# Stick-breaking attention inside a decoder layer: which short scans and which projection piece stand behind the current head's transpositions

## The chip, the cores and the metric

The kernel runs on one core of a Trainium2 chip. The metric is device time in microseconds (us) of one execution, as the median of several runs. Five engines work side by side, each through its own list of instructions in a fixed order: TensorE (PE in the profile; its weight loads are PEld), VectorE (DVE), ScalarE (ACT), GpSimd (POOL) and SyncE (SP), which issues the transfers. An instruction that waits holds up all that stand behind it in its engine's list.

## The reference

One layer of a hybrid decoder on 1024 positions of width 1024: a mixing sub-layer (stick-breaking attention with 16 heads of 64, a Mamba-2 mixer, two gates), a cross-attention into 256 memory tokens and a feed-forward. The change touches the stick-breaking attention alone:

```
z = einsum('bhtd,bhsd->bhts', q / 8, k)          # s < t only
log_1mb = where(causal, log_sigmoid(-z), 0)
tail = cumsum(log_1mb, axis=s, reverse=True)
w = where(causal, exp(z + tail), 0)
o = einsum('bhts,bhsd->bhtd', w, v)
```

With n = sigmoid(-z), the weight of a key s is the running product of n from the diagonal down to s+1, less the product down to s. So a query row needs one running product over its keys, taken from the diagonal towards key 0, and no logarithm.

## The kernel before

**Tiles.** A head's 1024 queries are eight blocks b = 0 to 7 of 128. Blocks 0 to 3 are the head's first half, 4 to 7 its second. Block b has keys 0 to 128(b+1). Per block, in `scores` (L923): TensorE multiplies queries and keys (L935, L936, tile `sc`), ScalarE takes the sigmoid into a tile `n` (L937), and VectorE runs one `tensor_tensor_scan` over the whole row in place (L939), 128 to 1024 elements long, so that a scan's width tells its block: 256 and 384 are blocks 1 and 2, 896 is block 6.

**Values.** For each half, `values` (L944) goes over key blocks i (4 in the first half, 8 in the second). `tr(i)` transposes the four query blocks' columns of key block i on TensorE into one PSUM tile `tr` of 512 columns (L953); ScalarE subtracts one and rounds to the high part `wth` (L956); VectorE makes the low part `wtl` (L957, kept in `lows[h, half, i]`). Three steps later `av(i)` adds both parts' products with the values into the PSUM tile `av` (L965, L966). After the last key block ScalarE copies `av` out (`oT`, L969).

**Buffers that bind.** There are two `tr` tiles, so `tr(2)` needs that `wtl` of key block 0 has read its tile. There is one `av` tile, so the first product of a half waits for the copy `oT` of the half before. In the first half the last key blocks hold only part of the queries: key block 2 is 256 wide and key block 3 is 128 wide.

**Projections.** Beside this, TensorE computes the q and k projections of heads further on, 128 columns at a time for two heads, in pieces of three matmuls of 512 columns (L126 to L128; `dense`, L847). A projection has sixteen pieces, eight for each half of the positions, and `(half, kk)` names one. The second half of an even head has the first eight pieces of a k projection beside it, that of an odd head the first eight of a q projection.

**Order.** The lists are not written in final order: the code is traced in the order that `interleave` (L983) gives, and a scheduler places the instructions, from due times and costs, under the ties that the code adds. `behind` (L218) ties an instruction's issue behind another of the same engine, and `issue_behind` (L213) adds such a tie afterwards. Two stand here before: each projection piece stands behind a product eight marks back (L861), and the scan of block 6 stands behind the low part of key block 2 of the same head's first half (L938). While a head's second half runs, VectorE also gets the scans of the next head's first half.

Of the kernel before, what the change touches and what calls it, by code (L numbers as in the profile page):

```python
# [16 lines left out]
P = 128  # L17
# [6 lines left out]
C_Q, C_K, C_V, C_Z = 0, 1024, 2048, 3072  # L24
# [30 lines left out]
def hybrid_block(ctx, tc, a, out, dbg=None):  # L55
    nc = tc.nc
    V, A, T = [InTurn(tc, e) for e in (nc.vector, nc.scalar, nc.tensor)]
# [12 lines left out]
    def mk(pl, shape, dt, tag, bufs=None):  # L70
        uid[0] += 1
        kw = {} if bufs is None else {"bufs": bufs}
        return pl.tile(shape, dt, tag=tag, name=f"{tag}_{uid[0]}", **kw)
# [57 lines left out]
    def load_split(wp, src, shape, rb=3, eng=None):  # L131
        raw = mk(wp, shape, F32, "wraw", bufs=rb)
        nc.sync.dma_start(raw, src)
        hi = mk(wp, shape, F32R, "whi")
        lo = mk(wp, shape, F32R, "wlo")
        hi_sb(hi, raw, eng)
        lo_of(lo, raw, hi)
        return hi, lo

    def colblock(w, c0, n=P):  # L140
        return w[:, c0:c0 + n].rearrange("(k p) f -> p k f", p=P)
# [3 lines left out]
    ident = mk(cp, [P, P], F32, "ident")  # L145
# [67 lines left out]
    def issue_behind(ins, mark):  # L213

        tc.add_manual_dep(ins.ins, mark.ins.name,
                          mybir.DependencyInfo(mybir.DependencyClass.NoSync, mybir.DependencyReason.DATA), reason="order")

    def behind(marks):  # L218

        st = ExitStack()  # L220
        for m in marks:
            st.enter_context(tc.issue_after(m.ins))
        return st
# [52 lines left out]
    with ExitStack() as pa:  # L276
# [24 lines left out]
        with ExitStack() as p1:  # L301
# [135 lines left out]
            pt = mk(psp, [P, HALF], F32, "pdt", bufs=1)  # L437
# [4 lines left out]
            pt = mk(psp, [P, HALF], F32, "pv")  # L442
# [382 lines left out]
        with ExitStack() as p2:  # L825
# [14 lines left out]
            V.memset(mask, 0.0)  # L840
            G.affine_select(mask[:, S - P:], mask[:, S - P:], [[-1, P]], ALU.is_gt, 1.0, base=0, channel_multiplier=1)

            marks, sig, highs, lows = [], [], [], {}
            PIN = 8
            FQ = 1

            def dense(c0, evac):  # L847

                st = {}

                def first():
                    st["w"] = load_split(wp, colblock(w_in, c0), [P, KT, P], 1)

                def part(half, kk):
                    def run():
                        if kk == 0:
                            st["ps"] = mk(psm, [P, HALF], F32, "mm")
                        whi, wlo = st["w"]
                        for k in range(kk * FQ, kk * FQ + FQ):
                            ins = mm3(st["ps"], whi[:, k, :], wlo[:, k, :], *hT(k, half), k == 0, k == KT - 1)  # L860
                            if k == kk * FQ and len(marks) >= PIN:  # L861
                                issue_behind(ins, marks[-PIN])
                        if kk == KT // FQ - 1:
                            evac(st["ps"], half)
                    return run

                return [first] + [part(half, kk) for half in range(2) for kk in range(KT // FQ)]
# [3 lines left out]
            def qk_proj(hp):  # L871
                for j in range(2):
                    heads[2 * hp + j] = {}

                def rooms(half, *names):
                    if half == 0:
                        for n in names:
                            for j in range(2):
                                heads[2 * hp + j][n] = mk(qk, [P, S], F32R, n)
                    sl = slice(half * HALF, (half + 1) * HALF)  # L880
                    return [heads[2 * hp + j][n][:, sl] for n in names for j in range(2)]

                def move(dst, src):
                    nc.sync.dma_start(dst.bitcast(F32), src.bitcast(F32))

                def ev_q(ps, half):
                    q0, q1 = rooms(half, "qs")
                    low = mk(t2, [P, HALF], F32R, "gt")  # L890
                    A.activation(q0, ps, AF.Copy)
                    A.activation(q1[HD:P], ps[HD:P], AF.Copy)
                    V.tensor_tensor(low, ps, q0.bitcast(F32), ALU.subtract)
                    move(q0[HD:P], low[0:HD])
                    move(q1[0:HD], low[HD:P])

                def ev_k(ps, half):
                    h0, h1, l0, l1 = rooms(half, "kh", "kl")
                    low = mk(t2, [P, HALF], F32R, "gt")
                    A.activation(h0, ps, AF.Copy)  # L900
                    A.activation(h1[HD:P], ps[HD:P], AF.Copy)
                    V.tensor_tensor(low, ps, h0.bitcast(F32), ALU.subtract)
                    move(h0[HD:P], h0[0:HD])
                    move(h1[0:HD], h1[HD:P])
                    for j, l in enumerate((l0, l1)):
                        for r in (l[0:HD], l[HD:P]):
                            move(r, low[j * HD:(j + 1) * HD])

                return dense(C_Q + hp * P, ev_q), dense(C_K + hp * P, ev_k)

            def gate_proj(gi):
                def ev(ps, half):
# [10 lines left out]
            def scores(h, half, tb, ns_):  # L923
                def run():
                    hd = heads[h]
                    if half == 0 and tb == 0:
                        values_of(h)
                    b = half * 4 + tb
                    L = (b + 1) * P
                    nt = mk(bp, [P, (half + 1) * HALF], F32, f"n{half}")  # L930
                    ns_.append(nt)
                    for s0 in range(0, L, HALF):
                        s1 = min(L, s0 + HALF)
                        ps = mk(psc, [P, HALF], F32, "sc")[:, :s1 - s0]
                        T.matmul(ps, hd["qs"][:, b * P:(b + 1) * P], hd["kh"][:, s0:s1], start=True, stop=False)  # L935
                        marks.append(T.matmul(ps, hd["qs"][:, b * P:(b + 1) * P], hd["kl"][:, s0:s1], start=False, stop=True))  # L936
                        sig.append(A.activation(nt[:, s0:s1], ps, AF.Sigmoid, scale=-(HD ** -0.5)))  # L937
                    with behind([lows[h, 0, 2]] if b == 6 else []):  # L938
                        V.tensor_tensor_scan(nt[:, 0:L][:, ::-1], nt[:, 0:L][:, ::-1], mask[:, S - L:][:, ::-1], 1.0, ALU.mult, ALU.max)  # L939
                return run  # L940

# [2 lines left out]
            def values(h, half, ns_):  # L944

                st = {}
                ni = 4 * (half + 1)

                def tr(i):
                    t0 = max(0, i - 4 * half)  # L950
                    pt = mk(pst, [P, HALF], F32, "tr")
                    for tb in range(t0, 4):
                        T.transpose(pt[:, tb * P:(tb + 1) * P], ns_[tb][:, i * P:(i + 1) * P], ident)  # L953
                    wh = mk(wt, [P, HALF], F32R, "wth")
                    wl = mk(wt, [P, HALF], F32R, "wtl")
                    highs.append(A.activation(wh[:, t0 * P:], pt[:, t0 * P:], AF.Identity, bias=mone))  # L956
                    lows[h, half, i] = V.scalar_tensor_tensor(wl[:, t0 * P:], pt[:, t0 * P:], -1.0, wh[:, t0 * P:].bitcast(F32), ALU.add, ALU.subtract)  # L957
                    st[i] = (wh, wl, t0 * P)

                def av(i):  # L960
                    if i == 0:
                        st["po"] = mk(psv, [P, HALF], F32, "av")
                    po, vt = st["po"], heads[h]["v"]
                    wh, wl, off = st[i]
                    T.matmul(po[:, off:], vt[:, i, :], wh[:, off:], start=i == 0, stop=False)  # L965
                    marks.append(T.matmul(po[:, off:], vt[:, i, :], wl[:, off:], start=False, stop=i == ni - 1))  # L966
                    if i == ni - 1:
                        o = mk(t2, [P, HALF], F32, "oT")
                        A.activation(o, po, AF.Copy)  # L969
                        for j in range(2):  # L970
                            nc.sync.dma_start(o_d[j][h * HD:(h + 1) * HD, half * HALF:(half + 1) * HALF], o[j * HD:(j + 1) * HD])

                def step(i):
                    def run():
                        if i < ni:
                            tr(i)
                        if i >= LAG:
                            av(i - LAG)
                    return run

                return [step(i) for i in range(ni + LAG)]
# [21 lines left out]
            ns_ = {m: [] for m in range(NM)}  # L1003
# [3 lines left out]
            for m in range(NM):  # L1007
                h, half = m // 2, m % 2
                hp, r = m // 4, m % 4
# [21 lines left out]
    with ExitStack() as p3:  # L1031
# [36 lines left out]
        marks = []  # L1068
# [411 lines left out]
    marks = []  # L1480
# [815 lines left out]
```

## Time and profile before

| | |
|---|---|
| median of 3 runs | 2502.8 us (2500.87 to 2503.42) |
| profiled execution, its own time from first to last instruction | 2498.5 us |
| attention stage, from the first scan to the last transposition | 660.4 to 1075.8 us of the span |
| two heads, from a scan of 896 at 851.64 us to the next but one at 901.06 us | 49.4 us |
| TensorE busy, 850 to 900 us | 48.71 of 50 us |
| VectorE busy, 850 to 900 us | 38.13 of 50 us |
| ScalarE busy, 850 to 900 us | 30.70 of 50 us |
| GpSimd busy, 850 to 900 us | 1.05 of 50 us |

The profiled execution has no time but its span; the runs' median lies 4.3 us above it. A row of the timeline gives start, length, engine, line, operation, the tile written and the tile read, the shapes, how many were merged, and in brackets how long the engine was idle before and what released it. Matmuls overlap: a 512-column matmul is listed with 0.39 us, and the next one starts 0.23 us after it. Instructions on VectorE and ScalarE also overlap by about 0.1 us.

### The profile page before, as it was taken

The numbers are of one execution on the slowest core, as the hardware profiler recorded it, in microseconds if no ns is written. First come the engines' busy times: TensorE is split into PE (matmuls) and PEld (weight loads), VectorE is DVE, ScalarE is ACT, GpSimd is POOL, SyncE is SP. The second block draws the span as 40 slices with busy tenths as digits, with TensorE's granted clock in tenths as the row PEclk, the third lists the DMA queues.
The fourth block names the chain that finished last, engine by engine and source line by source line (L and its number), as shares of the span: only waits on it lengthen the run. The fifth ranks groups of instructions, "written<-read, shape, count | busy, mean of one in ns | idle before, by whom it ended". The sixth has DMA issues, their size and how long they took to land. (4 is left out here: it accounts for less than half of the span.)

```text
span 2498.5 us, 33391 instructions
## 1 busy us (share of the span) xinstructions
PE 2438.4 (98%) x12306; PEld 2010.1 (80%) x12306; DVE 1807.4 (72%) x2261; ACT 1167.0 (47%) x2072; POOL 604.5 (24%) x505
## 2 busy tenths in 40 slices
PE   7999999999999999989999999999999999999998
PEld 5888788888788888877777778888888888888887
DVE  7767877767577777689888774577468556566997
ACT  5344455555465665566644312344335333344433
POOL 3221645443000000134444141102012322220001
PEclk9999999999999999999999999999999999999999
DMA  7565443333444334366332481321242322334322
GB/s 250 180 219 184 156 147 102 110 101 93 131 110 110 102 103 109 103 193 206 115 97 78 138 278 62 126 96 51 93 143 68 101 76 79 98 94 170 125 102 101
DMA packets 253741, 312.40 MB, mean 125 GB/s; under 512 B 17535, under 2 KB 169608, under 8 KB 253450
## 3 DMA queue, kind: packets, MB, share of 16 engines
q1 hardware_dynamic: 253290, 309.22, 38.8%
q8 instruction: 97, 1.59, 0.3%
q10 hardware_dynamic: 288, 1.05, 0.1%
q14 instruction: 66, 0.54, 0.1%
HBM read 210.59 MB, written 82.84 MB: 117 GB/s over the span
## 5 line engine op out<-in xcount | busy, mean ns | idle before, releaser
L939 DVE TENSOR_TENSOR_SCAN n<-n,mask 128x128 f32<-128x128 f32 (+7 forms) x128 | 170.0, 1350 | 27.7 <-ACT n L937 24.4
L123 DVE TENSOR_TENSOR sw<-sf,sw 128x512 fp32r<-128x512 f32 x142 | 127.0, 898 | 71.4 <-ACT sw L120 69.3
L120 ACT ACTIVATE sw<-sf 128x512 fp32r<-128x512 f32 x142 | 88.9, 628 | 157.4 <-PE mm L231 140.2
L956 ACT ACTIVATE wth<-tr,mone 128x512 fp32r<-128x512 f32 x192 | 110.7, 585 | 100.5 <-PE tr L953 100.1
L957 DVE SCALAR_TENSOR_TENSOR wtl<-tr,wth 128x512 fp32r<-128x512 f32 x192 | 101.8, 546 | 58.4 <-ACT wth L956 58.3
L732 DVE SCALAR_TENSOR_TENSOR b<-b,prmT,b 128x1023 f32<-128x1023 f32 (+2 forms) x72 | 110.5, 1534 | 16.9 <-ACT b L726 16.3
L123 DVE TENSOR_TENSOR sw<-wr,sw 128x512 fp32r<-128x512 f32 x107 | 98.8, 924 | 26.2 <-ACT sw L120 25.9
L230 PE MATMUL mm<-h,sw 128*128 128x512 f32 x288 | 112.0, 389 | 0.0
L231 PE MATMUL mm<-h,sw 128*128 128x512 f32 x288 | 111.7, 389 | 0.0
L116 POOL TENSOR_SCALAR whi<-wraw 128x1024 fp32r<-128x1024 f32 x13 | 14.8, 1136 | 395.0 <-PE mm L127 366.9
L229 PE MATMUL mm<-h,sw 128*128 128x512 f32 x288 | 109.9, 389 | 0.0
L197 POOL TENSOR_TENSOR sf<-wr,wr 128x512 f32<-128x512 f32 x36 | 53.1, 1476 | 228.8 <-DMA wr<-in_w_gu_dram 78.5
L126 PE MATMUL mm<-oth,bw 128*128 128x512 f32 x256 | 104.2, 407 | 4.2 <-DVE a L1289 2.6
L937 ACT ACTIVATE n<-sc 128x512 f32<-128x512 f32 (+1 forms) x192 | 86.7, 495 | 37.0 <-PE tr L953 20.6
L953 PE MATMUL tr<-ident,n 128*128 128x128 f32 x576 | 97.1, 275 | 6.1 <-DVE n L939 4.4
L128 PE MATMUL mm<-oth,bw 128*128 128x512 f32 x256 | 100.7, 393 | 0.0
L127 PE MATMUL mm<-otl,bw 128*128 128x512 f32 x256 | 100.6, 393 | 0.0
L128 PE MATMUL p<-bw,h 128*128 128x512 f32 x256 | 100.1, 392 | 0.5 <-DVE h L123 0.5
L174 POOL TENSOR_SCALAR rstd<-ms 128x1 f32<-128x1 f32 x74 | 28.0, 378 | 298.0 <-ACT x L181 226.8
L127 PE MATMUL p<-bw,h 128*128 128x512 f32 x256 | 99.9, 390 | 0.0
L126 PE MATMUL p<-bw,h 128*128 128x512 f32 x256 | 99.7, 390 | 0.0
L120 ACT ACTIVATE sw<-wr 128x512 fp32r<-128x512 f32 x107 | 67.1, 628 | 58.3 <-PE mm L231 51.4
(664 smaller groups left out, 7699.9 us busy)
## 6 DMA issues: line engine op xcount, KB each, us to landing
wr<-in_w_in_dram SPq DMA_DIRECT2D x36, 512.0 KB
wr<-in_w_gu_dram SPq DMA_DIRECT2D x72, 256.0 KB
zr<-in_w_in_dram SPq DMA_DIRECT2D x28, 512.0 KB
wraw<-in_w_in_dram SPq DMA_DIRECT2D x20, 512.0 KB
gu_d<-t SPq DMA_DIRECT2D x36, 256.0 KB
zs_d<-zo SPq DMA_DIRECT2D x32, 256.0 KB
dv_d<-v SPq DMA_DIRECT2D x16, 512.0 KB
xs_d<-b SPq DMA_DIRECT2D x32, 256.0 KB
```

The source lines that it names most:

```text
L120: A.activation(o, i, AF.Copy)
L123: return eng.tensor_tensor(o, i, hi.bitcast(F32), ALU.subtract)
L126: first = T.matmul(ps, sh, mh, start=start, stop=False)
L127: T.matmul(ps, sh, ml, start=False, stop=False)
L128: T.matmul(ps, sl, mh, start=False, stop=stop)
L229: T.matmul(ps, w[0][:, k, :], bh, start=first and k == 0, stop=False, skip_group_check=True)
L230: T.matmul(ps, w[0][:, k, :], bl, start=False, stop=False, skip_group_check=True)
L231: ins = T.matmul(ps, w[1][:, k, :], bh, start=False, stop=last and k == 3, skip_group_check=True)
L732: V.scalar_tensor_tensor(acc[:, sh:], y[:, :S - sh], cw(3 - sh, f), acc[:, sh:], ALU.mult, ALU.add)
L939: V.tensor_tensor_scan(nt[:, 0:L][:, ::-1], nt[:, 0:L][:, ::-1], mask[:, S - L:][:, ::-1], 1.0, ALU.mult, ALU.max)
L956: highs.append(A.activation(wh[:, t0 * P:], pt[:, t0 * P:], AF.Identity, bias=mone))
L957: lows[h, half, i] = V.scalar_tensor_tensor(wl[:, t0 * P:], pt[:, t0 * P:], -1.0, wh[:, t0 * P:].bitcast(F32), ALU.add, ALU.subtract)
```

## The change

Two ties are added. First, in `scores`, the scans of blocks 1 to 3 of every head but the first now stand behind the last low part (key block 3, 128 wide) of the first half of the head before; that is the head whose second half is being worked on when these scans are issued. Second, the piece (0, 5) of every k projection stands behind the last transposition of key block 1 of a second half, the latest one that the code has traced so far; `seconds` holds these.

```diff
-            marks, sig, highs, lows = [], [], [], {}
+            marks, sig, highs, seconds, lows = [], [], [], [], {}
...
-            def dense(c0, evac):
+            def dense(c0, evac, after=None):
...
                             if k == kk * FQ and len(marks) >= PIN:
                                 issue_behind(ins, marks[-PIN])
+                            if (half, kk) == after and seconds:
+                                issue_behind(ins, seconds[-1])
...
-                return dense(C_Q + hp * P, ev_q), dense(C_K + hp * P, ev_k)
+                return dense(C_Q + hp * P, ev_q), dense(C_K + hp * P, ev_k, (0, 5))
...
-                    with behind([lows[h, 0, 2]] if b == 6 else []):
+                    with behind([lows[h, 0, 2]] if b == 6 else [lows[h - 1, 0, 3]] if h > 0 and 0 < b < 4 else []):
                         V.tensor_tensor_scan(nt[:, 0:L][:, ::-1], nt[:, 0:L][:, ::-1], mask[:, S - L:][:, ::-1], 1.0, ALU.mult, ALU.max)
...
-                        T.transpose(pt[:, tb * P:(tb + 1) * P], ns_[tb][:, i * P:(i + 1) * P], ident)
+                        turned = T.transpose(pt[:, tb * P:(tb + 1) * P], ns_[tb][:, i * P:(i + 1) * P], ident)
+                    if half == 1 and i == 1:
+                        seconds.append(turned)
```

No instruction is added or removed on any engine, and the lists of ScalarE, GpSimd and SyncE stay as they were.

The first place is VectorE at the start of a second half, here head 4; `n_1263` and `n_1272` are blocks 1 and 2 of head 5, `n_1235` is block 6 of head 4, `n_1280` is block 3 of head 5. Before:

```order
L893 TENSOR_TENSOR gt_6791<-mm_6689,qs_6675 128x512
L939 SCALAR_TENSOR_TENSOR n_1263_6851<-n_1263_6851,mask_5385 128x256
L939 SCALAR_TENSOR_TENSOR n_1272_6883<-n_1272_6883,mask_5385 128x384
L957 SCALAR_TENSOR_TENSOR wtl_6740<-tr_6736,wth_6739 128x256
L939 SCALAR_TENSOR_TENSOR n_1235_6746<-n_1235_6746,mask_5385 128x896
L957 SCALAR_TENSOR_TENSOR wtl_6759<-tr_6756,wth_6758 128x128
L939 SCALAR_TENSOR_TENSOR n_1280_6914<-n_1280_6914,mask_5385 128x512
L957 SCALAR_TENSOR_TENSOR wtl_6815<-tr_6809,wth_6814 128x512
```

And in the changed kernel, where the line numbers are two to four higher:

```order
L895 TENSOR_TENSOR gt_6791<-mm_6689,qs_6675 128x512
L961 SCALAR_TENSOR_TENSOR wtl_6740<-tr_6736,wth_6739 128x256
L941 SCALAR_TENSOR_TENSOR n_1235_6746<-n_1235_6746,mask_5385 128x896
L961 SCALAR_TENSOR_TENSOR wtl_6759<-tr_6756,wth_6758 128x128
L941 SCALAR_TENSOR_TENSOR n_1263_6851<-n_1263_6851,mask_5385 128x256
L941 SCALAR_TENSOR_TENSOR n_1272_6883<-n_1272_6883,mask_5385 128x384
L941 SCALAR_TENSOR_TENSOR n_1280_6914<-n_1280_6914,mask_5385 128x512
L961 SCALAR_TENSOR_TENSOR wtl_6815<-tr_6809,wth_6814 128x512
```

The scans of 256 and 384 go from before the low part of key block 2 to behind that of key block 3, so the scan of 896 comes two scans earlier; the scan of 512 and all behind it keep their places. This happens thirteen times, in the second halves of heads 1 to 13. In head 0 the list had that order already.

The second place is TensorE at the start of an even head's second half, again head 4: `mm_6818` is the k projection of heads further on, `tr_6809` and `tr_6830` are the transpositions of key blocks 0 and 1, `sc_6996` is a score of the next head. Before:

```order
L126 MATMUL mm_6818<-b21h_118,whi_6805 128x512
L127 MATMUL mm_6818<-b21l_119,whi_6805 128x512
L128 MATMUL mm_6818<-b21h_118,wlo_6806 128x512
L953 MATMUL tr_6809<-ident_89,n_1235_6746 128x128
L953 MATMUL tr_6809<-ident_89,n_1242_6771 128x128
L966 MATMUL av_6762<-wtl_6759,v_6552 128x128
L953 MATMUL tr_6830<-ident_89,n_1223_6702 128x128
L953 MATMUL tr_6830<-ident_89,n_1229_6723 128x128
L953 MATMUL tr_6830<-ident_89,n_1235_6746 128x128
L953 MATMUL tr_6830<-ident_89,n_1242_6771 128x128
L965 MATMUL av_6869<-wth_6814,v_6552 128x512
```

And in the changed kernel:

```order
L938 MATMUL sc_6996<-kl_6402,qs_6134 128x512
L955 MATMUL tr_6809<-ident_89,n_1235_6746 128x128
L955 MATMUL tr_6809<-ident_89,n_1242_6771 128x128
L970 MATMUL av_6762<-wtl_6759,v_6552 128x128
L955 MATMUL tr_6830<-ident_89,n_1223_6702 128x128
L955 MATMUL tr_6830<-ident_89,n_1229_6723 128x128
L955 MATMUL tr_6830<-ident_89,n_1235_6746 128x128
L955 MATMUL tr_6830<-ident_89,n_1242_6771 128x128
L126 MATMUL mm_6818<-b21h_118,whi_6805 128x512
L127 MATMUL mm_6818<-b21l_119,whi_6805 128x512
L128 MATMUL mm_6818<-b21h_118,wlo_6806 128x512
L969 MATMUL av_6869<-wth_6814,v_6552 128x512
```

The three matmuls of piece (0, 5) go from before the second pair of transpositions of key block 0 to behind those of key block 1, directly before the half's first product. The score pair that ends with `sc_6996`, which stood ahead of piece (0, 4), now stands behind it. This happens in the even heads 2 to 12; in head 0 only the three matmuls move.

## The prediction

> **What bounds the kernel now.** I read the page's totals first, then the busy time of a stretch of the attention stage, then who waited for whom there (columns: us in total, times, longest), then the timeline of two heads row by row.
>
> ```profile
> span 2498.5 us, 33391 instructions
> ...
> 850.00:900.00 50.00, 48.71 (x268) 40.71 (x267) 38.13 (x48) 30.70 (x63) 1.05 (x1) 1.00 0.39 107
> ```
>
> ```profile
> PE av L965 <- ACT oT L969: 4.5, 6, 0.7
> PE tr L953 <- DVE n L939: 3.8, 7, 0.6
> ```
>
> In 50 us of attention TensorE is busy for 48.71, at full granted clock (1.00), while VectorE has 38.13. So TensorE bounds the stage, and what can be won is its idle time. The waits (690 to 1010 us) name all of that: seven times a transposition waited for a scan, six times the first product of a half for the copy `oT`. That is one stall a head. It comes where a second half begins: in odd heads the first kind, in even heads the second. The change moves work on VectorE at these thirteen places.
>
> **Odd heads.** Head 7, TensorE, VectorE and ScalarE:
>
> ```profile
> 852.76 0.40 PE L128 MATMUL mm<-b11h,wlo 128*128 128x512 f32 x1
> 853.71 0.44 PE L953 MATMUL tr<-ident,n 128*128 128x128 f32 x2 [0.55 <-DVE n L939]
> ...
> 856.83 0.60 PE L953 MATMUL tr<-ident,n 128*128 128x128 f32 x4
> ```
>
> ```profile
> 849.88 1.53 DVE L939 TENSOR_TENSOR_SCAN n<-n,mask 128x256 f32<-128x256 f32 x2
> 851.32 0.40 DVE L957 SCALAR_TENSOR_TENSOR wtl<-tr,wth 128x256 fp32r<-128x256 f32 x1
> 851.64 2.02 DVE L939 TENSOR_TENSOR_SCAN n<-n,mask 128x896 f32<-128x896 f32 x1
> ...
> 853.75 1.21 DVE L939 TENSOR_TENSOR_SCAN n<-n,mask 128x512 f32<-128x512 f32 x1
> 854.90 0.69 DVE L957 SCALAR_TENSOR_TENSOR wtl<-tr,wth 128x512 fp32r<-128x512 f32 x1
> ```
>
> ```profile
> 849.11 0.48 ACT L956 ACTIVATE wth<-tr,mone 128x256 fp32r<-128x256 f32 x1
> ```
>
> **Even heads.** Head 8, in the same order of engines:
>
> ```profile
> 878.90 0.39 PE L126 MATMUL mm<-b21h,whi 128*128 128x512 f32 x1
> ...
> 879.35 0.40 PE L128 MATMUL mm<-b21h,wlo 128*128 128x512 f32 x1
> 879.59 0.38 PE L953 MATMUL tr<-ident,n 128*128 128x128 f32 x2
> ...
> 881.23 0.50 PE L965 MATMUL av<-wth,v 128*128 128x512 f32 x1 [0.74 <-ACT oT L969]
> 881.57 0.60 PE L953 MATMUL tr<-ident,n 128*128 128x128 f32 x4
> ```
>
> ```profile
> 874.49 0.68 DVE L893 TENSOR_TENSOR gt<-mm,qs 128x512 fp32r<-128x512 f32 x1
> 875.09 1.53 DVE L939 TENSOR_TENSOR_SCAN n<-n,mask 128x256 f32<-128x256 f32 x2
> 876.54 0.40 DVE L957 SCALAR_TENSOR_TENSOR wtl<-tr,wth 128x256 fp32r<-128x256 f32 x1
> 876.85 2.01 DVE L939 TENSOR_TENSOR_SCAN n<-n,mask 128x896 f32<-128x896 f32 x1
> 878.78 0.27 DVE L957 SCALAR_TENSOR_TENSOR wtl<-tr,wth 128x128 fp32r<-128x128 f32 x1
> 878.96 1.21 DVE L939 TENSOR_TENSOR_SCAN n<-n,mask 128x512 f32<-128x512 f32 x1
> 880.73 0.69 DVE L957 SCALAR_TENSOR_TENSOR wtl<-tr,wth 128x512 fp32r<-128x512 f32 x1 [0.55 <-ACT wth L956]
> ```
>
> ```profile
> 875.08 0.74 ACT L956 ACTIVATE wth<-tr,mone 128x256 fp32r<-128x256 f32 x2
> ...
> 880.01 0.69 ACT L956 ACTIVATE wth<-tr,mone 128x512 fp32r<-128x512 f32 x1 [3.70 <-PE tr L953]
> 880.59 0.59 ACT L969 ACTIVATE oT<-av 128x512 f32<-128x512 f32 x1
> ```
>
> **The change in odd heads.** The lost time is counted from start to start: after a 512-column matmul a transposition follows in 879.59 - 879.35 = 0.24 us where nothing is waited for, and in the odd head in 853.71 - 852.76 = 0.95. So 0.71 us is lost, more than the 0.55 in the bracket, which counts from the listed end. The Trainium skill, Perfetto Trace Analysis, section Tensor Engine Instruction (MATMUL, LD_WEIGHTS), says that a matmul's reported end is worked out from its size and not observed; the trace agrees, since matmuls of 0.39 us start 0.23 apart. By the brackets the six full odd heads below would give 3.3 us instead of 4.3, and the whole 4.4 instead of 5.4.
>
> Now the scans of 256 and 384 stand behind. The low part of key block 2 comes first, at 849.88; its high part ended at 849.11 + 0.48 = 849.59, so nothing is waited for. The scan of 896 follows after 851.64 - 851.32 = 0.32, at 850.20, and ends at 852.22. TensorE wants it at 852.76 + 0.24 = 853.00: the stall is gone, with 0.78 to spare. What is late next is the low part of key block 0, which must have read its `tr` tile before the transpositions of key block 2. VectorE has the same work up to there and was not idle, so that low part stays at 854.90 and ends at 855.59. TensorE, 0.71 earlier, wants the tile at 856.83 - 0.71 = 856.12. The copy `oT` depends on TensorE and moves along. So 0.71 us is won, in heads 1, 3, 5, 7, 9 and 11: 4.26 us. The last odd head has no scores between:
>
> ```profile
> 1005.89 0.69 DVE L957 SCALAR_TENSOR_TENSOR wtl<-tr,wth 128x512 fp32r<-128x512 f32 x1
> ```
>
> ```profile
> 1007.12 0.60 PE L953 MATMUL tr<-ident,n 128*128 128x128 f32 x4
> ```
>
> The low part ends at 1006.58. In the even head these transpositions start 881.57 - (880.73 + 0.69) = 0.15 after it, so here not before 1006.73: 0.39 us won. Odd heads together: 4.65 us.
>
> The two deferred scans are wanted first when the next head's own first half is transposed, after the whole of this second half; putting them off by three rows costs nothing.
>
> **The change in even heads.** On TensorE the three matmuls of piece (0, 5), 879.59 - 878.90 = 0.69 us, go behind the transpositions of key block 1 (the score pair that changes places with piece (0, 4) is ahead of them before and after), so those transpositions, the high part and `oT` all come 0.69 earlier (high part 879.32 to 880.01, `oT` 879.90 to 880.49), and the matmuls fill the wait for `oT`. If nothing else held, 0.69 us would be won.
>
> But VectorE holds. Its low part of key block 2 now comes first and needs a high part that starts at 875.08 here, behind the evacuations of the q projection, and ends 0.48 later at 875.56. VectorE, free at 875.09, stands idle until about 875.59 (a hand-over takes 880.73 - 880.70 = 0.03): 0.50 us, and the two scans that could fill it are queued behind. Then:
> - scan of 896: 875.59 + (876.85 - 876.54) = 875.90, to 877.91; TensorE wants it at 879.59 - 0.69 = 878.90, in time;
> - low part of key block 3: + 1.93 = 877.83; the two scans: + 0.18 = 878.01; the scan of 512: + (876.54 - 875.09) = 879.46;
> - low part of key block 0: + (854.90 - 853.75) = 880.61.
>
> That is 0.12 earlier than the 880.73 of before. The transpositions of key block 2, which already stood directly behind that low part (881.42, then 881.57), come at 881.45. The 0.62 us for which VectorE waited here (878.96 + 1.15 = 880.11, to 880.73) is eaten by the 0.50 at the front. So 0.12 us is won, in six even heads 0.72 us, and the rest of TensorE's stall changes its releaser from `oT` to the low part.
>
> Head 0 shows this price, because its list had the new order of VectorE already:
>
> ```profile
> 682.88 1.26 DVE L957 SCALAR_TENSOR_TENSOR wtl<-tr,wth 128x512 fp32r<-128x512 f32 x2
> ```
>
> ```profile
> 683.60 0.66 PE L953 MATMUL tr<-ident,n 128*128 128x128 f32 x4 [0.32 <-DVE wtl L957]
> ```
>
> The low part starts directly behind the scans and the transpositions wait for it. Moving piece (0, 5) ahead of that wait moves nothing on VectorE: nothing won in head 0.
>
> **Sum.** 4.26 + 0.39 + 0.72 = 5.4 us (5.37): the profiled 2498.5 becomes 2493.1. The runs' median stands 4.3 above that span, and I keep this difference: 2502.8 - 5.4 = 2497.4. No queue of transfers is passed by anything. What could not be read is how the even heads' order on VectorE runs. Its bounds are 0.69 won, where the low part comes in time, and a loss, where the wait at the front grows past 0.62; I take 0.12, since every row of the chain is there.
>
> **Rivals.**
> - *The even heads win in full.* For it: the waits name `oT` and not the low part. Against it: the transpositions already start within 0.15 of the low part's end. If the high part of key block 2 came 0.5 earlier, the low part of key block 0 would come at 880.11 and no longer decide: 4.65 + 6 x 0.69 = 8.8 us, 2494.0.
> - *Handed back.* TensorE's 0.71 in odd heads is met by a VectorE or ScalarE chain later in the same head that did not move. For it: VectorE has 38.13 of 50 us and gets its scans in bursts. Against it: after the low part of key block 0 all rows of VectorE wait for things that TensorE makes. Left over are the even heads' 0.72: 2502.1.
> - *Slower: VectorE blocked at the front.* The low part of key block 2 waits longer than in head 8, with the scans behind it. Such waits of low parts for high parts are the commonest of VectorE's:
>
> ```profile
> DVE wtl L957 <- ACT wth L956: 42.7, 62, 1.8
> ```
>
> At the longest, 1.8 us in each even head, the low part of key block 0 would come 1.8 - 0.62 = 1.18 later than before: 6 x 1.18 - 4.65 = 2.4 us lost, 2505.2. It decides from 0.62 on in the even heads, and from 0.62 + 4.65 / 6 = 1.4 on the whole is slower. Against it: the high part hangs on ScalarE's order, which does not change. The Trainium skill, in the same section, calls ScalarE, VectorE and GpSimd strict first-in first-out; this is the rule that speaks against tying work behind a low part, and head 0 agrees.
>
> **How the numbers follow.** The forecast has a chance of 0.57, the full win 0.14, handed back 0.21, slower 0.08. The forecast's own range, by the spread of the runs shown (2500.87 to 2503.42), is 2496.0 to 2499.0. For 8 in 10 I reach from the full win's 2494.0, less half a microsecond, to 2502.3 just past handed back. A change under 0.2%, 5.0 us, can't be told from none with this kernel. The forecast lies at that edge (2497.8), so its chance falls half and half: faster 0.30 + 0.14 and some of the forecast's upper side, 0.47; same 0.27 + 0.21, 0.48; slower 0.05, since the slow case mostly stays within 0.2%.
>
> **What would show it.** Right: in odd heads TensorE's wait for the scan is gone; in even heads its wait for `oT` shrinks to some 0.2 and a wait for the low part of about half a microsecond stands at the transpositions of key block 2; VectorE waits 0.5 before the low part of key block 2 in even heads and nowhere else there; two heads take 49.4 - 0.8 = 48.6 us. Wrong: an even head without wait behind `oT` (full win), a new TensorE wait of 0.3 or more in odd heads (handed back), or waits of VectorE at the front above 0.62.

## The result, and the profile after

| | before | changed |
|---|---|---|
| median, first comparison (8 runs each) | 2502.78 us | 2495.43 us |
| ratio of the runs, 95% interval | | 0.9971 (0.9962 to 0.9981) |
| median, repeated beside the last experiments (17 and 11 runs) | 2501.22 us | 2495.48 us |
| ratio, 95% interval | | 0.9977 (0.9968 to 0.9986) |
| profiled span | 2498.5 us | 2494.5 us |
| first to last transposition of the attention stage | 410.8 us | 405.3 us |

Runs at a lowered granted clock are not counted: two of the kernel before in the repeated comparison (2784 and 3041 us, clocks 0.83 and 0.75) and one of the scans' tie alone below (4667 us, clock 0.87). The changed kernel is faster, by 0.29% when first measured and by 0.23% when repeated. The stage's length, read in one trace each, settles more than the medians do. It stands in the list of one line's instructions, which gives shortest, median and longest duration in ns and then the first and the last start. Before, and changed:

```profile
L953 PE MATMUL tr<-ident,n x576: 270/272/330, 665.0 to 1075.8; 128*128 128x128 f32 x192
```

```profile
L955 PE MATMUL tr<-ident,n x576: 270/272/329, 666.6 to 1071.9; 128*128 128x128 f32 x192
```

So the stage became 5.5 us shorter. In the changed kernel's execution it also began 1.6 us later, though nothing ahead of it was changed, which is why the span shows only 4.0. The busy times shortly before the stage show where most of this lies (the columns are those of the prediction's row, the third from the end is TensorE's granted clock); before, and changed:

```profile
644.00:648.50 4.50, 3.50 (x15) 2.92 (x16) 1.64 (x3) 1.37 (x3) 0.00 (x0) 1.00 0.66 189
644.00:648.50 4.50, 3.35 (x9) 2.69 (x10) 1.79 (x3) 1.52 (x3) 0.00 (x0) 0.62 0.64 174
```

In this execution of the changed kernel the granted clock averaged 0.62 over these 4.5 us, and TensorE ran 9 matmuls in them instead of 15; six matmuls at 0.23 apart are 1.4 us, by estimate.

The page's first line, TensorE's busy time in the same 50 us as before (49.70 now, 48.71 then), and its waits from 690 to 1008 us:

```profile
span 2494.5 us, 33391 instructions
```

```profile
850.00:900.00 50.00, 49.70 (x275) 41.58 (x275) 38.87 (x49) 30.09 (x62) 1.05 (x1) 1.00 0.42 113
```

```profile
PE tr L955 <- DVE wtl L961: 1.6, 6, 0.3
PE sc L938 <- DMA kl<-gt: 0.6, 1, 0.6
```

The seven waits for a scan and the six for `oT` are gone from the list. In their place stand six waits for a low part, and one wait for a transfer. (The list leaves out short waits: some 0.2 us for `oT` is still there, as the even head below shows.)

**An odd head after** (head 7 again), TensorE and VectorE:

```profile
851.98 0.39 PE L128 MATMUL mm<-b11h,wlo 128*128 128x512 f32 x1
852.21 0.38 PE L955 MATMUL tr<-ident,n 128*128 128x128 f32 x2
...
852.87 0.48 PE L126 MATMUL mm<-b21h,whi 128*128 128x512 f32 x1
...
855.27 0.49 PE L955 MATMUL tr<-ident,n 128*128 128x128 f32 x3
```

```profile
849.10 0.42 DVE L961 SCALAR_TENSOR_TENSOR wtl<-tr,wth 128x256 fp32r<-128x256 f32 x1
849.43 2.02 DVE L941 TENSOR_TENSOR_SCAN n<-n,mask 128x896 f32<-128x896 f32 x1
851.36 0.27 DVE L961 SCALAR_TENSOR_TENSOR wtl<-tr,wth 128x128 fp32r<-128x128 f32 x1
851.54 2.65 DVE L941 TENSOR_TENSOR_SCAN n<-n,mask 128x256 f32<-128x256 f32 x3
854.10 1.26 DVE L961 SCALAR_TENSOR_TENSOR wtl<-tr,wth 128x512 fp32r<-128x512 f32 x2
```

The transposition follows the matmul after 0.23 us where it was 0.95. The scan of 896 ends at 851.45, 0.76 before it is wanted; the walk had 0.78. The low part of key block 0 starts 4.67 after the scan of 896, and TensorE wants its tile 5.84 after it, in time.

**An even head after** (head 8), in the order TensorE, VectorE, ScalarE:

```profile
878.56 0.40 PE L128 MATMUL mm<-b21h,wlo 128*128 128x512 f32 x1
879.00 0.50 PE L969 MATMUL av<-wth,v 128*128 128x512 f32 x1
879.77 0.66 PE L955 MATMUL tr<-ident,n 128*128 128x128 f32 x4 [0.27 <-DVE wtl L961]
880.18 0.48 PE L970 MATMUL av<-wtl,v 128*128 128x512 f32 x1
```

```profile
872.93 0.68 DVE L895 TENSOR_TENSOR gt<-mm,qs 128x512 fp32r<-128x512 f32 x1
874.03 0.42 DVE L961 SCALAR_TENSOR_TENSOR wtl<-tr,wth 128x256 fp32r<-128x256 f32 x1 [0.42 <-ACT wth L960]
874.37 2.02 DVE L941 TENSOR_TENSOR_SCAN n<-n,mask 128x896 f32<-128x896 f32 x1
...
876.49 2.64 DVE L941 TENSOR_TENSOR_SCAN n<-n,mask 128x256 f32<-128x256 f32 x3
879.05 1.26 DVE L961 SCALAR_TENSOR_TENSOR wtl<-tr,wth 128x512 fp32r<-128x512 f32 x2
```

```profile
873.52 0.73 ACT L960 ACTIVATE wth<-tr,mone 128x256 fp32r<-128x256 f32 x2
...
878.36 0.59 ACT L973 ACTIVATE oT<-av 128x512 f32<-128x512 f32 x1
```

VectorE stands idle for 0.42, as listed, before the low part of key block 2, for the high part that begins at 873.52. From start to start it is 0.50: the low part comes 874.03 - 872.93 = 1.10 after the evacuation ahead of it (L895, at 872.93), where 0.60 is usual (875.09 - 874.49 before the change). Then its chain runs without a gap to the low part of key block 0 at 879.05, and the transpositions at 879.77 wait for that. `oT` ends at 878.95, and the product follows it at 879.00, 0.21 later than a matmul follows a matmul (0.44 for 0.23).

### The profile page after: what moved, and what is told of

It is laid out like the page before. It is cut to its first block, busy times and chain, and to the rows that moved or that the text cites. A ratio compares the mean times of both kernels' runs of the same rounds, so it can differ in the third digit from the quotient of the medians.

```text
span 2494.5 us, 33391 instructions
## 1 busy us (share of the span) xinstructions
PE 2440.2 (98%) x12306; PEld 2009.7 (81%) x12306; DVE 1805.9 (72%) x2261; ACT 1166.4 (47%) x2072; POOL 604.1 (24%) x505
```

## The experiments

Each kernel differs from the changed one in its ties alone, so all compute the whole layer; but where ties differ, the scheduler may place other instructions differently too, and this is said where it happened. The diffs are against the changed kernel, with `...` where lines are left out. "Two heads" is from the scan of 896 of head 7 to that of head 9, and "stage" from the first to the last transposition, each in one trace.

| kernel | two heads | stage | ratio to before, interval |
|---|---|---|---|
| before | 49.42 | 410.8 | |
| changed | 48.44 | 405.3 | 0.9971 (0.9962 to 0.9981) |
| changed, again | 48.41 | 405.3 | 0.9977 (0.9968 to 0.9986) |
| scans' tie alone | 48.56 | 406.5 | 0.9984 (0.9975 to 0.9993) |
| piece's tie alone | 48.82 | 406.9 | 0.9987 (0.9978 to 0.9995) |
| scans' tie in odd heads, piece's tie | 48.02 | 403.2 | 0.9969 (0.9958 to 0.9981) |
| scan of 256 untied, piece's tie | 47.92 | 401.5 | 0.9969 (0.9956 to 0.9981) |
| high part ahead of the sigmoids, both ties | 47.97 | 402.5 | 0.9969 (0.9959 to 0.9980) |
| scan of 256 untied, scan of 512 later | 47.97 | 401.2 | 0.9967 (0.9955 to 0.9980) |

**The scans' tie alone.**

```diff
-                return dense(C_Q + hp * P, ev_q), dense(C_K + hp * P, ev_k, (0, 5))
+                return dense(C_Q + hp * P, ev_q), dense(C_K + hp * P, ev_k)
```

> The scans' tie alone; piece (0, 5) is where it was. Theory A (the prediction's walk): odd heads win 0.71 each as in the changed kernel; in even heads TensorE still does piece (0, 5) before the second pair of transpositions, so the high part and oT come as late as before, and nothing is won there: two heads 49.42 - 0.71 = 48.7 us, the whole 4.65 us under the kernel before, 0.7 over the changed kernel. Rival B (the scans' tie also relieves even heads): 48.5 us or less for two heads, as fast as the changed kernel. Rival C (the tie costs in even heads where nothing fills the wait): 49.0 or more.

TensorE's waits in this kernel, and its transpositions:

```profile
PE av L969 <- ACT oT L973: 4.4, 6, 0.7
PE sc L938 <- DMA kl<-gt: 0.7, 2, 0.4
```

```profile
L955 PE MATMUL tr<-ident,n x576: 269/273/332, 666.3 to 1072.8; 128*128 128x128 f32 x192
```

The waits for scans are gone and the six for `oT` stand as before (4.5 us then). The score pair of the even heads moved behind piece (0, 4) here too, although piece (0, 5) stayed; with the piece's tie alone it doesn't move. So that move belongs to the scans' tie, not to the piece's. The stage is 4.3 us shorter than before with 0.7 us of waits for transfers in it; the walk gave 4.65. The two heads came out at 48.56, between A's 48.7 and B's 48.5, so they don't separate these two; the waits do, since the even heads' stall is whole. C fell.

**The piece's tie alone.**

```diff
-                    with behind([lows[h, 0, 2]] if b == 6 else [lows[h - 1, 0, 3]] if h > 0 and 0 < b < 4 else []):
+                    with behind([lows[h, 0, 2]] if b == 6 else []):
```

> The piece's tie alone; all scans are where they were. Theory A: in even heads the scan of 896 ends at 878.87 in the time of the kernel before, just when TensorE wants it (878.90), and VectorE, not held at the front, starts the low part of key block 0 at 880.11 instead of 880.73: 0.62 us won in each of six even heads, nothing in odd ones: two heads 48.8 us, 3.7 us under the kernel before. This would say that in even heads the scans' tie takes back what the piece's tie gives. Rival B (the piece wins only with the scans out of its way): two heads 49.3 us or more, the time of the kernel before.

TensorE's waits and transpositions, and VectorE in head 8:

```profile
PE tr L955 <- DVE n L941: 3.8, 7, 0.5
```

```profile
L955 PE MATMUL tr<-ident,n x576: 269/273/331, 665.1 to 1072.0; 128*128 128x128 f32 x192
```

```profile
876.95 1.22 DVE L941 TENSOR_TENSOR_SCAN n<-n,mask 128x512 f32<-128x512 f32 x1
878.10 0.69 DVE L961 SCALAR_TENSOR_TENSOR wtl<-tr,wth 128x512 fp32r<-128x512 f32 x1
```

Two heads take 48.82 and the stage is 3.9 us shorter, as A said. The low part of key block 0 follows the scan of 512 with no wait, 1.15 after its start (1.77 before the change), and the wait for `oT` is out of the list. So the piece alone wins 0.6 in an even head, and both ties together won 0.25 there: the parts, 4.3 and 3.9, add to 8.2, and together they gave 5.5.

**The scans' tie in odd heads only, with the piece's tie.**

```diff
-                    with behind([lows[h, 0, 2]] if b == 6 else [lows[h - 1, 0, 3]] if h > 0 and 0 < b < 4 else []):
+                    with behind([lows[h, 0, 2]] if b == 6 else [lows[h - 1, 0, 3]] if h > 0 and h % 2 == 0 and 0 < b < 4 else []):
```

> Both ties, but the scans' tie only for scans that are issued during odd heads. Theory A: both gains at once, 0.71 in odd and 0.62 in even heads: two heads 48.1 us, 8.4 us under the kernel before and 3.0 under the changed kernel; VectorE has no wait at the front of even heads. Rival B (the even heads' stall has another cause than VectorE's 0.50 us at the front): 48.5 us, as the changed kernel.

```profile
PE sc L938 <- DMA kl<-gt: 0.7, 1, 0.7
PE sc L937 <- DMA kh<-kh: 0.2, 1, 0.2
```

These are all of TensorE's listed waits from 690 to 1008 us in this kernel, and VectorE doesn't wait at the front of even heads. The score pair of the even heads stands where it stood before the change. Two heads take 48.02 for A's 48.1. The stage is 7.6 us shorter than before, with 0.9 us of waits for transfers in it.

**The scan of 256 untied, with both other ties.**

```diff
-                    with behind([lows[h, 0, 2]] if b == 6 else [lows[h - 1, 0, 3]] if h > 0 and 0 < b < 4 else []):
+                    with behind([lows[h, 0, 2]] if b == 6 else [lows[h - 1, 0, 3]] if h > 0 and 1 < b < 4 else []):
```

> Both ties, but the scan of 256 (block 1) is not tied in any head, so it stands ahead of the low part of key block 2 and fills VectorE's 0.50 us there; TensorE's list is that of the changed kernel. Theory A: same gains as with ties in odd heads only, 0.71 and 0.62: two heads 48.1 us, 8.4 us under the kernel before. Rival B: 48.5 us as the changed kernel. Rival C (the scan of 896 comes late in odd heads, 0.6 us later than in the changed kernel): the wait of a transposition for a scan is back in odd heads; by the walk there is 0.78 us to spare, less 0.60.

Head 8 in this kernel, VectorE and TensorE:

```profile
871.21 0.68 DVE L941 TENSOR_TENSOR_SCAN n<-n,mask 128x256 f32<-128x256 f32 x1
871.81 0.40 DVE L961 SCALAR_TENSOR_TENSOR wtl<-tr,wth 128x256 fp32r<-128x256 f32 x1
872.12 2.02 DVE L941 TENSOR_TENSOR_SCAN n<-n,mask 128x896 f32<-128x896 f32 x1
...
876.21 0.67 DVE L961 SCALAR_TENSOR_TENSOR wtl<-tr,wth 128x512 fp32r<-128x512 f32 x1
```

```profile
876.68 0.51 PE L969 MATMUL av<-wth,v 128*128 128x512 f32 x1
877.02 0.60 PE L955 MATMUL tr<-ident,n 128*128 128x128 f32 x4
877.38 0.48 PE L970 MATMUL av<-wtl,v 128*128 128x512 f32 x1
```

```profile
L955 PE MATMUL tr<-ident,n x576: 269/273/329, 666.3 to 1067.8; 128*128 128x128 f32 x192
```

The scan of 256 takes 0.60 and fills the time for which VectorE stood idle; the low part of key block 2 follows without a wait. The transpositions of key block 2 follow the product after 0.34 instead of 0.77, and TensorE has no listed wait from 690 to 1008 us, so rival C's wait for a scan didn't come back. The lists of TensorE and ScalarE are those of the changed kernel; only VectorE's order differs. Of the 3.8 us between the stages (405.3 and 401.5), 2.6 lie in the six even heads, 0.43 each, and 0.7 in head 3, where the changed kernel's execution waited for a transfer and this one did not. The stage is 9.3 us shorter than before; the walk had 8.4. This kernel's median was 2493.03 beside 2501.55 for the kernel before on that chip. That it beats the changed kernel too is shown by the stage alone: the two intervals in the table overlap.

**The changed kernel again.**

> The changed kernel itself, timed again beside the two that follow. First measured, its runs lay 7.4 us under the kernel before, while its attention stage (first to last transposition) was 5.49 us shorter in the trace. Theory A (the ties win what the stage shows, the rest is spread between executions): 4 to 7 us under the kernel before, the stage again 405.3 +- 0.8. Rival B (2 us are won outside the stage): again 7 us or more, and the trace shorter by 1 us or more outside the stage.

```profile
L955 PE MATMUL tr<-ident,n x576: 270/272/331, 666.9 to 1072.2; 128*128 128x128 f32 x192
```

The stage repeats at 405.3, and the medians lie 0.23% apart, 5.7 us (3.5 to 8.0), inside A. Outside the stage this trace is not shorter than that of the kernel before but 3.7 us longer (2496.7 less 405.3, against 2498.5 less 410.8), which speaks against B, though the interval alone would still allow its 7 us.

**The high part ahead of the sigmoids.**

```diff
-            marks, sig, highs, seconds, lows = [], [], [], [], {}
+            marks, sig, highs, seconds, lows, wths = [], [], [], [], {}, {}
...
-                        sig.append(A.activation(nt[:, s0:s1], ps, AF.Sigmoid, scale=-(HD ** -0.5)))
+                        with behind([wths[h - 1, 0, 2]] if h > 0 and 0 < b < 3 else []):
+                            sig.append(A.activation(nt[:, s0:s1], ps, AF.Sigmoid, scale=-(HD ** -0.5)))
...
+                    wths[h, half, i] = highs[-1]
```

> The changed kernel with one tie more: the sigmoids of the next head's blocks 1 and 2 stand behind the high part of key block 2 on ScalarE, so that this high part no longer waits for them; VectorE's list is that of the changed kernel. Theory A (the even heads are held by the 0.50 us for which VectorE waits for this high part at the front): that wait goes, the low part of key block 0 comes 0.5 earlier in six even heads: the stage 405.3 - 3.0 = 402.3 us, 3 us less than the changed kernel in the same call. Rival B (the even heads are held by the order on VectorE itself, whatever comes first): 405.3. Rival C (the sigmoids, now later, hold score tiles, and TensorE waits for those): the front's wait is gone but the stage is not shorter, and score matmuls wait for ScalarE.

Head 8 in this kernel, ScalarE and VectorE:

```profile
871.77 0.47 ACT L961 ACTIVATE wth<-tr,mone 128x256 fp32r<-128x256 f32 x1
872.15 0.76 ACT L940 ACTIVATE n<-sc 128x256 f32<-128x256 f32 x2
```

```profile
871.83 0.68 DVE L895 TENSOR_TENSOR gt<-mm,qs 128x512 fp32r<-128x512 f32 x1
872.43 0.41 DVE L963 SCALAR_TENSOR_TENSOR wtl<-tr,wth 128x256 fp32r<-128x256 f32 x1
```

```profile
L956 PE MATMUL tr<-ident,n x576: 270/272/329, 666.7 to 1069.2; 128*128 128x128 f32 x192
```

VectorE keeps the changed kernel's order, but the high part ends at 872.24 and the low part starts directly behind the instruction ahead of it, 0.60 after that one's start. The stage is 402.5, 2.8 us shorter than the changed kernel's; A had 3.0. TensorE's list isn't quite the changed kernel's here: a product of 256 columns moved up in each head, and in even heads a score pair of 128 columns, all of them ahead of the stall. So this kernel alone wouldn't settle the cause; the one before, with only VectorE's order different, does, and both agree: filling VectorE's idle time and taking away what made it wait each won 0.43 in an even head.

**The scan of 512 later as well.**

```diff
-                    with behind([lows[h, 0, 2]] if b == 6 else [lows[h - 1, 0, 3]] if h > 0 and 0 < b < 4 else []):
+                    with behind([lows[h, 0, 2]] if b == 6 else [lows[h - 1, 1, 0]] if h > 0 and b == 3 else [lows[h - 1, 0, 3]] if h > 0 and b == 2 else []):
```

> As the kernel that leaves the scan of 256 untied, and the scan of 512 (block 3) tied behind the low part of key block 0 of the second half, so that this low part no longer stands behind it. Theory A (with the front's wait filled, TensorE's own work and oT set the even heads, and the low part of key block 0 only by 0.1 or so): the stage within 1 us of the 401.5 of the kernel without the tie of 256; head 0 wins 0.3 and head 13 0.3, while in even heads the scan of 512 now pushes the low part of key block 1. Rival B (the low part of key block 0 still sets the pace everywhere): 3 us or more shorter than 401.5. Rival C (the scan of 512 in its new place makes the low part of key block 1 late): 2 us or more longer.

```profile
877.94 0.69 DVE L961 SCALAR_TENSOR_TENSOR wtl<-tr,wth 128x512 fp32r<-128x512 f32 x1 [1.02 <-ACT wth L960]
878.55 1.21 DVE L941 TENSOR_TENSOR_SCAN n<-n,mask 128x512 f32<-128x512 f32 x1
```

VectorE now waits 1.02 us in this even head for the high part, so TensorE's and ScalarE's part comes last, and the stage is 401.2 (668.7 to 1069.9) against 401.5. With the idle time filled, VectorE's order no longer decides in the even heads, which take 24.0 to 24.1 us in both kernels. In head 0 it still did: its part of the stage became 0.8 us shorter, where A had 0.3, and slightly longer steps elsewhere, most of all into heads 3 and 13 where TensorE waited for transfers, took back 0.5. So the sum fits A better than its parts do.

## Why the prediction was right, point by point

- **What bounds the stage.** TensorE's idle time was what could be won. Where a wait went from its list, the stage became shorter by about its size: by 3.9 us with the six waits for `oT` gone (4.5 listed), by 4.3 with the seven for scans gone (3.8 listed) and 0.7 of new waits.
- **The terms.** The time from the first transposition of key block 2 in one head's second half to that of the next head is a head's step. The steps in the traces of before and after, in us, beside the prediction's terms:

| step into | before | changed | won in all | forecast |
|---|---|---|---|---|
| heads 1, 5, 7, 11 | 24.65 to 24.75 | 23.93 to 23.99 | 2.97, 0.74 each | 2.84, 0.71 each |
| heads 3 and 9 | 24.94, 24.64 | 24.79, 24.17 | 0.62 | 1.42 |
| even heads 2 to 12 | 24.72 to 24.75 | 24.46 to 24.50 | 1.49, 0.25 each | 0.72, 0.12 each |
| head 13 | 26.73 | 26.21 | 0.52 | 0.39 |
| head 14 | 30.50 | 30.60 | -0.10 | nothing |
| stage | 410.8 | 405.3 | 5.5 | 5.4 |

For heads 7 and 8 the steps can be read from the starts of the transpositions in the rows shown, with these two for head 6, before and changed:

```profile
832.16 0.60 PE L953 MATMUL tr<-ident,n 128*128 128x128 f32 x4
831.34 0.66 PE L955 MATMUL tr<-ident,n 128*128 128x128 f32 x4 [0.27 <-DVE wtl L961]
```

- **Odd heads, 0.71 each.** The mechanism was right, and the size too where nothing else came in: 856.83 - 832.16 = 24.67 became 855.27 - 831.34 = 23.93. The stall itself gave 0.72 (0.95 to 0.23). The rows behind it also became quicker, as they weren't interrupted. Before, the next projection piece started at

```profile
854.43 0.48 PE L126 MATMUL mm<-b21h,whi 128*128 128x512 f32 x1
```

  which is 0.72 after the transposition at 853.71; after, it is 852.87 - 852.21 = 0.66. But the same price is paid behind the even head's new wait: there the four transpositions take 880.18 - 879.77 = 0.41 until the next product, against 877.38 - 877.02 = 0.36 where the wait is filled. The two about cancel. The start-to-start count, and not the bracket's 0.55, gave the right size.
- **Even heads, 0.12 each.** The step on which the forecast turned was right in its mechanism, and its size was half of what came. The walk on VectorE came out to the hundredth: the low part of key block 0 starts 879.05 - 872.93 = 6.12 after the evacuation (L895), and 880.73 - 874.49 = 6.24 before. What was misread is the last step. The prediction let the transpositions stand 0.15 behind the low part's end, as they did before. But there they were held by the product ahead of them (881.57 - 881.23 = 0.34, the same 0.34 as with the scan of 256 untied), not by the low part. Where they do wait for it they follow its end (879.71 in the trace) by 0.06, so 0.09 more was won, and the low part itself was 0.03 shorter. Head 0, the prediction's own example of this wait, has the same 0.06 in the trace of before. The waits are the ones named: 0.21 at the product, and at the transpositions 0.77 - 0.34 = 0.43 for the "about half" expected.
- **The last odd head, head 0.** Head 13 won 0.52 for 0.39; the 0.15 misread above is in that term too. Head 0 won nothing, as forecast: from its first transposition to key block 2 it takes 18.60 in both traces.
- **What was missing.** I held that no queue of transfers is passed by anything, and put waits for transfers at nothing. One came:

```profile
757.00 0.39 PE L938 MATMUL sc<-kl,qs 128*128 128x512 f32 x1
758.02 0.30 PE L938 MATMUL sc<-kl,qs 128*128 128x128 f32 x1 [0.63 <-DMA kl<-gt]
```

  In head 3's second half a score waited for a copy of the k projection's low part, and head 3 won 0.15 instead of 0.71. Head 9 lost 0.24 at the same kind of matmul without a releaser in the trace. The wait in head 3 was 0.63, 0.34 when the same kernel was run again, 0.44 with the scans' tie alone, 0.74 with that tie in odd heads only, 0.30 and 0.15 in the last two kernels, and none with the piece's tie alone or with the scan of 256 untied. In the latter TensorE comes to that place no later, so being earlier isn't the whole cause; what decides when the copy lands is not shown.
- **Sum.** 5.4 forecast, 5.5 in the stage, and that this agrees so well is partly luck: the even heads and head 13 won 0.9 more than forecast, the odd heads 3 and 9 won 0.8 less. In the medians it is 7.4 and then 5.7, with the forecast inside both intervals. The measured 2495.4 lies 2.0 below the 2497.4 forecast and 0.6 below the forecast's own range; it is inside the range for 8 in 10. The stage accounts for 5.5 of the first 7.4.
- **What was kept from the trace of before.** I kept 4.3 us between the span and the median. In all other runs on record the time lies 1.7 to 1.8 above the span, so the execution profiled before was a short one of its kind, some 2.5 under the median. This cost the forecast nothing, because both sides were taken from the runs.
- **The chances.** I held that under 0.2% can't be told from none. The two ties alone lie at 0.16% and 0.13%, and neither interval in the table reaches 1. The 0.47 for faster also has 0.03 in it that the forecast's and the full win's shares don't give (0.30 + 0.14).
- **The rivals.** The full win in even heads needed the high part of key block 2 half a microsecond earlier; the experiment that brings it earlier won 2.8 us, near the 6 x 0.5 that follows. Handed back came in part: a new wait above 0.3 in an odd head was its sign, and head 3 shows one, but for a transfer and not for a chain of VectorE or ScalarE. The slower case needed more than 0.62 at the front, and it was 0.50.

## What to carry to other kernels

Before tying work behind an instruction, look at what that instruction itself waits for: the tie turns its wait into idle time of the whole engine. Where two ties at one place are each worth something, time each alone, because one can use up the slack that the other needs; here 4.3 and 3.9 us alone gave 5.5 together, and leaving one scan of 0.6 us untied gave 9.3. Read a TensorE stall from start to start of the matmuls around it, and take the price of a hand-over only from rows in which that hand-over is what was waited for.

## What the runs showed of the hardware

After a stall of TensorE the next transpositions run slower than in an unbroken row: 0.72 to 0.73 us instead of 0.66 for the same seven matmuls, in all six odd heads, so a stall costs a little more than its own length. Outside the changed stage, executions differ by more than this change's smaller terms: from the last transposition to the end it is 1422.6 us in one execution of the changed kernel and 1424.5 in another, while the stage itself repeated within 0.1. In the longer one the granted clock averaged 0.57 from 1450.5 to 1454.5 us of the span; in the shorter one it was 1.00 there.
